# Moving the GpSimd share of the experts' weight subtractions into VectorE's queue

## The chip, the cores and the metric

The kernel runs on one core of one Trainium2 chip. The metric is the device time of one execution in microseconds (us), as a median over runs. The engines are TensorE (PE; its weight loads are PEld), VectorE (DVE), ScalarE (ACT), GpSimd (POOL) and SyncE (SP), which issues most of the DMAs.

## What is computed

The reference is one layer of a hybrid decoder: four kinds of token mixers over 2048 tokens of width 1024, a projection with a layer norm, and then a mixture of experts. The change lies in the experts alone. Each token goes to 2 of 32 SwiGLU experts (width 512), and what they give is weighted and added to the token's row:

```python
def expert_block(args):
    xb, e = args
    return (jax.nn.silu(xb @ w_gate[e]) * (xb @ w_up[e])) @ w_down[e]

y_rows = lax.map(expert_block, (x_rows, block_expert)).reshape(n_rows, d)
y = jax.ops.segment_sum(y_rows * row_gate[:, None], row_tok, num_segments=t_tok + 1)[:t_tok]
```

All data are 32-bit floats.

## The kernel before, in words

The kernel keeps its accuracy with split operands: a float operand is written as a high part `h`, the operand rounded to TensorE's float32r form, and a low part `l = raw - h`, and a product takes three matmuls (high by high, high by low, low by high). For every piece of an expert's weights somebody therefore has to make `h` by a rounding copy (ScalarE) and `l` by a subtraction. The change is about who subtracts.

The mixers, the output projection and the routing take the first two thirds of the time and know nothing of the change. Then `moe` (L1934) runs over the 32 experts in the order of `ORDER`. The weights of one expert come in six raw pieces of 1 MB, each 128 partitions by 2 x 1024 floats: four of gate and up together (`raw_gu`, L1813, two DMAs of 512 KB) and two of the down matrix (`raw_dn`, L1822, one DMA). Raw pieces lie in a pool of five buffers (`m_raw`, L1806). `split_piece` (L1832) handles a piece in two halves of 128x1024: the copy on ScalarE (L1835), then the subtraction on the engine that it is given (L1836). The gate/up parts go to a pool of eight buffers (`m_g`, L1382), which is `h` and `l` of four pieces and so one expert; the down parts go to two buffers each of `m_dh` and `m_dl` (L1807), also one expert. So a piece of the next expert can be split only when TensorE is done with that of the present one.

`load_g` (L1964) lets the last of its pieces be subtracted on GpSimd and the others on VectorE; `load_d` (L1969) lets the first of its two be subtracted on VectorE and the second on GpSimd. An expert thus has eight subtractions on VectorE (six gate/up, two down) and four on GpSimd (two and two). For the first expert two gate/up pieces are prepared earlier, with the routing.

The tokens of an expert are handled in blocks of 128. The first block is always computed; the second under an `If` on the count (over 128), with fewer matmuls when it is at most half full; a third is rare (`third`, L2009, under the `If` of L2011, which TensorE, ScalarE, VectorE and GpSimd all go through). Per expert: the gathered rows are turned by TensorE and split (`transpose_split`, L1400; the transposes are L1408, the split is a ScalarE copy at L51 and a VectorE subtraction at L52, whose input is in PSUM), multiplied with gate and up (`moe_gu`, matmuls L1884), passed through the activation (`moe_h`: ScalarE L1900, VectorE L1901 and L1902; the halves of the second block are folded together before, L1892 and L1893), turned and split again, and multiplied with the down weights (`moe_dn`, matmuls L1916), one expert late. The result is copied out by ScalarE (L1923), with a VectorE step for the second block (L1925), and added to the rows in memory by an indirect storing DMA (`moe_put`, L1930). These stores and the gathers of rows (`moe_gather`, L1840) are issued by GpSimd, in whose queue the subtractions stand too.

The order of the calls in `moe` isn't the order of the queues. When the program is built, the framework's scheduler puts each engine's instructions into an order of its own, by priorities and by its own estimates; nothing moves into or out of an `If`. In the profile the subtractions of L1836 therefore stand between the activation's steps and the splits.

Of the kernel before, what the change touches and what calls it, by code (L numbers as in the profile page):

```python
# [30 lines left out]
class Layer:  # L31
# [1902 lines left out]
    def moe(self, G0=(), x0=None, experts=32):  # L1934
        nc, tc, NB = self.nc, self.tc, self.NB
# [22 lines left out]
        GW, DW, H, Y, cnt = {}, {}, {}, {}, {}  # L1958
# [5 lines left out]
        def load_g(e):  # L1964
            done = list(G0) if e == 0 else []
            R = [self.raw_gu(e, k) for k in range(len(done), 4)]
            GW[e] = done + [self.split_piece((self.g_tile(), self.g_tile()), r, nc.gpsimd if i == len(R) - 1 else nc.vector) for i, r in enumerate(R)]

        def load_d(e):  # L1969
            R = [self.raw_dn(e, k) for k in range(2)]  # L1970
            DW[e] = [self.split_piece(self.d_tiles(), r, g) for r, g in zip(R, (nc.vector, nc.gpsimd))]

        def gather0(e):
            if e < experts:
# [55 lines left out]
        def counts(e):  # L2030
            if e % 4 == 0:
                for t, k, g in ((self.turn_cnt, "pe", [ET.PE]), (self.turn_cnt, "pool", [ET.Pool]), (self.turn_max, "four", FOUR)):
                    for i, v in enumerate(load_counts(t, e, g)):
                        cnt[e + i, k] = v

        load_g(0)
        counts(0)
        if not x0:
# [6 lines left out]
        for e in range(experts):  # L2045
            counts(e + 1)
            if e > 1:
                put1(e - 2)
            third(e - 1)
            gather(e + 1)  # L2050
            gather0(e + 1)
            self.moe_gu(x0, GW[e], b0)
            with tc.If(cnt[e, "pe"] > 128):
                sized(e, 1, lambda s: self.moe_gu(x1, GW[e], b1, half=s))
            H[e, 0] = self.moe_h(b0, gate(e, 0))
            self.fold(b1, half(e, 1))
            H[e, 1] = self.moe_h(b1, gate(e, 1))
            if e + 1 < experts:
                x0 = self.turned(X[0])
                load_g(e + 1)  # L2060
            if e == 31:
                self.lx, self.lp, self.lt = {}, {}, {}
                self.late_x(T - self.LATE)
            if e:
                down0(e - 1, ht[0])
            h0 = turn(e, 0)
            if e:
                down1(e - 1, ht[1])
            ht = h0, turn(e, 1)
            if e + 1 < experts:  # L2070
                x1 = self.turned(X[1], spread=True)
            load_d(e)
        e, t = experts - 1, T - self.LATE
# [316 lines left out]
```

## Time and profile before

| | us |
|---|---|
| median of three runs | 3057.15 (3054.57 to 3073.09) |
| the profiled execution | 3065.59 |
| its span, first to last instruction | 3063.8 |
| of it before the experts | 1975 |
| the experts' stage | 995 |
| behind them (last norm and output) | 94 |

The profile is of one execution. Times in its rows count from the start of the span. "Busy" is the time in which an engine executes; an idle stretch is put down to what ended it. PEclk is the granted share of TensorE's clock, 1.00 for 2.4 GHz and 0.50 for 1.2 GHz.

### The profile page before, as it was taken

What the parts mean: (1) busy time and instruction counts of PE and PEld (TensorE: products, weight loads), DVE (VectorE), ACT (ScalarE), POOL (GpSimd) and SP (SyncE); (2) the same over time, 40 slices, a digit from 0 to 9 for tenths busy, and PEclk for the clock granted to TensorE, in tenths of its full rate; (3) what the DMA queues carried; (4) which work ended last, traced back from release to release, by engine and by line L of the source; (5) the groups of instructions that cost most, each with busy time, mean ns of one, the idle gap of its engine ahead of it and who ended that gap; (6) DMA issues with size and microseconds to landing.
All of it is one profiled execution on the core that took longest, in us unless ns stands there. A gap on an engine that the chain in (4) does not pass through costs nothing. (4 is left out here: it accounts for less than half of the span.)

```text
span 3063.8 us, 42798 instructions
## 1 busy us (share of the span) xinstructions
PE 2826.6 (92%) x15420; PEld 2225.7 (73%) x15421; DVE 1934.6 (63%) x4061; ACT 1225.6 (40%) x2003; POOL 887.9 (29%) x552
## 2 busy tenths in 40 slices
PE   8999999999989999999999999898899888999866
PEld 6898877777867766665577799776677767777644
DVE  6366365366555567776646735677677866667868
ACT  4222132222124423333311112265576656566854
POOL 1000000011010023334431101445464544546524
PEclk9999999999989898989999999999999999999988
DMA  6332242121125422110243412377597767877865
GB/s 189 100 102 71 69 125 70 55 73 56 53 50 164 158 79 80 50 38 18 83 141 136 143 69 70 114 276 259 182 309 233 251 230 230 264 246 244 286 223 195
DMA packets 287042, 442.98 MB, mean 145 GB/s; under 512 B 84088, under 2 KB 152040, under 8 KB 286760
## 3 DMA queue, kind: packets, MB, share of 16 engines
q1 hardware_dynamic: 272200, 397.78, 39.2%
q0 software_dynamic: 14560, 41.47, 5.4%
q8 instruction: 172, 2.82, 0.4%
q14 instruction: 110, 0.90, 0.1%
HBM read 350.52 MB, written 96.50 MB: 146 GB/s over the span
## 5 line engine op out<-in xcount | busy, mean ns | idle before, releaser
L1884 PE MATMUL m_g<-m_g,xhl 128*128 128x512 f32 x2032 | 521.0, 404 | 16.4 <-PEq L2011 9.1
L1884 PEld LDWEIGHTS m_g<-m_g,xhl 128*128 128x128 f32 x2032 | 376.0, 192 | 110.1 <-issue 31.5
L1836 DVE TENSOR_TENSOR m_g<-m_raw,m_g 128x1024 fp32r<-128x1024 f32 x188 | 273.5, 1482 | 109.7 <-ACT m_g L1835 104.4
L1835 ACT CAST m_g<-m_raw 128x1024 fp32r<-128x1024 f32 x252 | 255.4, 1058 | 111.2 <-PEq L2011 99.2
L1916 PE MATMUL m_y<-m_dh,m_h 128*128 128x512 f32 x656 | 225.8, 409 | 24.0 <-PEq L2011 7.3
L59 PE MATMUL pbank<-xh,wh 128*128 128x512 f32 x544 | 226.6, 417 | 6.6 <-DVE us L213 3.6
L60 PE MATMUL pbank<-xl,wh 128*128 128x512 f32 x544 | 218.8, 402 | 0.0
L61 PE MATMUL pbank<-xh,wl 128*128 128x512 f32 x544 | 218.3, 402 | 0.0
L51 ACT CAST xhl<-bank 128x512 fp32r<-128x512 f32 x204 | 118.3, 609 | 240.2 <-PE bank L1408 239.1
L1836 POOL TENSOR_TENSOR m_g<-m_raw,m_g 128x1024 fp32r<-128x1024 f32 x64 | 184.9, 2971 | 84.5 <-ACT m_g L1835 47.5
L1466 PE MATMUL wide<-wt,xhl 128*128 128x512 f32 x768 | 183.2, 397 | 3.6 <-ACT xhl L51 3.6
L1836 POOL TENSOR_TENSOR m_dl<-m_raw,m_dh 128x1024 fp32r<-128x1024 f32 x64 | 178.3, 2819 | 23.9 <-ACT m_dh L1835 23.7
L1304 POOL TENSOR_TENSOR mla_acc<-mla_acc,mla_pt 128x512 f32<-128x512 f32 (+3 forms) x112 | 132.2, 1180 | 147.4 <-ACT mla_pt L1302 137.4
L1466 PEld LDWEIGHTS wide<-wt,xhl 128*128 128x128 f32 x768 | 143.9, 189 | 40.0 <-ACT xhl L51 7.5
L1302 ACT ACTIVATE mla_pt<-sbank 128x512 f32<-128x512 f32 (+3 forms) x160 | 85.3, 533 | 212.6 <-PE sbank L1298 110.8
L1916 PEld LDWEIGHTS m_y<-m_dh,m_h 128*128 128x128 f32 x656 | 128.6, 196 | 57.1 <-issue 10.8
L52 DVE TENSOR_TENSOR xhl<-bank,xhl 128x512 fp32r<-128x512 f32 x204 | 136.2, 684 | 49.9 <-ACT xhl L51 48.0
L1930 POOL DMA_INDIRECT accd<-m_y,m_put x47 | 96.1, 2044 | 247.2 <-ACT m_y L1923 148.1
L59 PE MATMUL pbank<-wh,xh 128*128 128x256 f32 x512 | 151.8, 296 | 0.0
L1646 PE MATMUL gate<-wt,xhl 128*128 128x354 f32 (+1 forms) x864 | 150.3, 331 | 1.1 <-ACT xhl L51 0.9
L60 PE MATMUL pbank<-wl,xh 128*128 128x256 f32 x512 | 150.3, 293 | 0.0
L61 PE MATMUL pbank<-wh,xl 128*128 128x256 f32 x512 | 149.1, 291 | 0.0
(643 smaller groups left out, 6279.6 us busy)
## 6 DMA issues: line engine op xcount, KB each, us to landing
m_raw<-in_moe_w_down SPq DMA_DIRECT2D x64, 1024.0 KB
m_raw<-in_moe_w_gate SPq DMA_DIRECT2D x126, 512.0 KB
m_raw<-in_moe_w_up SPq DMA_DIRECT2D x126, 512.0 KB
wraw<-in_w_in SPq DMA_DIRECT2D x80, 256.0 KB
o_x<-in_x SPq DMA_DIRECT2D x16, 512.0 KB
x1d<-m_g SPq DMA_DIRECT2D x16, 512.0 KB
accd<-wide SPq DMA_DIRECT2D x16, 512.0 KB
m_raw<-accd SPq DMA_DIRECT2D x7, 1024.0 KB
```

The source lines that it names most:

```text
L51: nc.scalar.copy(hi, src)
L52: (eng and nc.gpsimd or nc.vector).tensor_sub(lo, src, hi.bitcast(F32))
L59: nc.tensor.matmul(out, lh, rh, start=start, stop=False)
L60: nc.tensor.matmul(out, lh, rl, start=False, stop=False)
L61: nc.tensor.matmul(out, ll, rh, start=False, stop=stop)
L1304: (nc.vector if kt in self.SUMS else nc.gpsimd).tensor_add(acc[:, c0 * 128:512], acc[:, c0 * 128:512], pt[:, 0:n])
L1466: nc.tensor.matmul(p[:, j], a[:, k], W[k][bb][:, j * 512:j * 512 + 512], start=k == 0 and i == 0, stop=k == 7 and i == 2)
L1646: nc.tensor.matmul(p[:, 0:n], a[:, k], b[:, o:o + n], start=k == 0 and i == 0, stop=k == 7 and i == 2)
L1835: self.nc.scalar.copy(h[:, i], raw[:, i])
L1836: lo_eng.tensor_sub(l[:, i], raw[:, i], h[:, i].bitcast(F32))
L1884: self.mark["pe"] = self.nc.tensor.matmul(banks[:, j], a, b[:, k % 2, j * 512:j * 512 + 512], start=k == 0 and i == 0, stop=k == 7 and i = ...
L1916: self.nc.tensor.matmul(p[:, j], a, b[:, k % 2, j * 512:j * 512 + 512], start=k == 0 and i == 0, stop=k == 3 and i == len(ps) - 1)
```

## The change

All subtractions of the experts' weights go to VectorE: of the last gate/up piece and of the second down piece too. GpSimd keeps the gathers and the adding stores. Nothing else differs.

```diff
         def load_g(e):
             done = list(G0) if e == 0 else []
             R = [self.raw_gu(e, k) for k in range(len(done), 4)]
-            GW[e] = done + [self.split_piece((self.g_tile(), self.g_tile()), r, nc.gpsimd if i == len(R) - 1 else nc.vector) for i, r in enumerate(R)]
+            GW[e] = done + [self.split_piece((self.g_tile(), self.g_tile()), r, nc.vector) for r in R]
 
         def load_d(e):
             R = [self.raw_dn(e, k) for k in range(2)]
-            DW[e] = [self.split_piece(self.d_tiles(), r, g) for r, g in zip(R, (nc.vector, nc.gpsimd))]
+            DW[e] = [self.split_piece(self.d_tiles(), r, nc.vector) for r in R]
```

## Rows read from the trace of the kernel before

**Rows 1.** Stages; from:to, length, busy of PE, PEld, DVE, ACT, POOL, clock, DMA.
```profile
0.00:1975.00 1975.00, 1888.17 (x11204) 1482.50 (x11205) 1156.10 (x3166) 551.18 (x1072) 342.85 (x315) 0.95 0.29 89
1975.00:2970.00 995.00, 884.11 (x4000) 699.65 (x4000) 707.69 (x741) 636.33 (x858) 506.68 (x223) 0.96 0.76 250
2970.00:3063.80 93.80, 54.28 (x216) 43.58 (x216) 70.83 (x157) 38.07 (x74) 38.37 (x16) 0.77 0.55 200
```
**Rows 2.** Groups of the experts' stage; shape, count, busy us, mean ns, idle before and releasers.
```profile
L1836 DVE TENSOR_TENSOR m_g<-m_raw,m_g 128x1024 fp32r<-128x1024 f32 x188 | 273.5, 1482 | 109.7 <-ACT m_g L1835 104.4 <-PE bank L1408 3.2 <-DVEq L2011 1.9
L1835 ACT CAST m_g<-m_raw 128x1024 fp32r<-128x1024 f32 x252 | 255.4, 1058 | 111.2 <-PEq L2011 99.2 <-DMA m_raw<-in_moe_w_down 9.2 <-DMA m_raw<-in_moe_w_up 1.2
...
L1836 POOL TENSOR_TENSOR m_g<-m_raw,m_g 128x1024 fp32r<-128x1024 f32 x64 | 184.9, 2971 | 84.5 <-ACT m_g L1835 47.5 <-issue 37.0
L1836 POOL TENSOR_TENSOR m_dl<-m_raw,m_dh 128x1024 fp32r<-128x1024 f32 x64 | 178.3, 2819 | 23.9 <-ACT m_dh L1835 23.7
...
L1836 DVE TENSOR_TENSOR m_dl<-m_raw,m_dh 128x1024 fp32r<-128x1024 f32 x64 | 114.3, 1786 | 12.3 <-ACT m_dh L1835 12.3
...
L1916 PEld LDWEIGHTS m_y<-m_dl,m_h 128*128 128x128 f32 x360 | 71.0, 197 | 15.3 <-POOL m_dl L1836 1.3
```
**Rows 3.** The subtraction's line, whole run; count, then duration ns least, median, most.
```profile
L1836 DVE TENSOR_TENSOR m_g<-m_raw,m_g x188: 1205/1220/6290, 1983.0 to 2915.4; 128x1024 fp32r<-128x1024 f32 x188
```
**Rows 4.** VectorE's timeline; start, duration, line, count merged: free, then held.
```profile
2406.46 3.49 DVE L1836 TENSOR_TENSOR m_g<-m_raw,m_g 128x1024 fp32r<-128x1024 f32 x3
...
2600.09 8.49 DVE L1836 TENSOR_TENSOR m_g<-m_raw,m_g 128x1024 fp32r<-128x1024 f32 x3
2608.51 0.68 DVE L52 TENSOR_TENSOR m_h<-bank,m_h 128x512 fp32r<-128x512 f32 x1
```
**Rows 5.** GpSimd's timeline in the same stretch.
```profile
2602.20 5.29 POOL L1836 TENSOR_TENSOR m_g<-m_raw,m_g 128x1024 fp32r<-128x1024 f32 x2
```
**Rows 6.** TensorE's timeline; in brackets the idle time before and what ended it.
```profile
2082.95 0.66 PE L1408 MATMUL bank<-ident,m_t 128*128 128x128 f32 x4 [1.85 <-DVE xhl L52]
...
2609.24 1.12 PE L1408 MATMUL bank<-ident,m_xg 128*128 128x128 f32 x4 [4.24 <-DVE m_h L52]
...
2922.31 0.66 PE L1408 MATMUL bank<-ident,m_xg 128*128 128x128 f32 x4 [1.66 <-DVE m_h L52]
```
**Rows 7.** Stretches of half clock behind a wait, columns as in the stages.
```profile
2361.70:2368.50 6.80, 5.67 (x18) 4.82 (x19) 5.91 (x8) 4.90 (x7) 2.77 (x2) 0.50 0.69 233
...
2849.80:2853.20 3.40, 3.40 (x13) 2.87 (x12) 3.31 (x5) 2.18 (x4) 0.00 (x0) 0.50 0.93 290
```
**Rows 8.** Waits of TensorE's weight loads, experts' stage; us in total, times, longest.
```profile
PEld m_g L1884 <- POOL m_g L1836: 4.3, 7, 0.9
```
**Rows 9.** Stretches of one expert each, columns as in the stages.
```profile
2220.80:2245.00 24.20, 23.31 (x112) 18.49 (x111) 19.05 (x22) 18.66 (x25) 15.92 (x8) 1.00 0.90 290
2245.00:2265.70 20.70, 19.89 (x93) 14.81 (x91) 19.79 (x22) 18.27 (x26) 13.02 (x6) 1.00 0.97 313
...
2592.70:2619.70 27.00, 22.17 (x94) 16.98 (x93) 21.85 (x21) 17.57 (x26) 13.36 (x6) 0.87 0.76 259
...
2743.50:2777.70 34.20, 33.64 (x157) 27.25 (x155) 21.53 (x22) 18.38 (x26) 18.84 (x9) 1.00 0.89 296
...
2830.00:2859.20 29.20, 21.49 (x93) 16.13 (x92) 25.27 (x22) 17.51 (x25) 15.40 (x7) 0.94 0.89 283
...
2881.80:2902.50 20.70, 19.81 (x94) 14.96 (x92) 19.78 (x22) 18.28 (x26) 13.85 (x6) 1.00 0.87 301
```
**Rows 10.** Gathers, who waited for them, landings; then the stores.
```profile
L1840 POOL DMA_INDIRECT m_xg<-x1d,m_idx x46: 937/993/1822, 1976.4 to 2883.5; - x46
...
  PE bank L1408: 4.0, 1
...
DMA to landing us min/median/max: 4.2/7.0/10.6
...
L1930 POOL DMA_INDIRECT accd<-m_y,m_put x47: 1562/2106/2687, 2029.3 to 2968.6; - x47
```
**Rows 11.** The subtractions alone, one expert; length, busy of DVE and POOL.
```profile
2245.00:2265.70 20.70, 11.03 (x8) 9.19 (x4) 1.00 0.97 313
```

## The prediction

> **What bounds the kernel now.** I read the stages first. The experts' stage, 1975 to 2970 us, holds TensorE for 884.1 of its 995 us, VectorE for 707.7, ScalarE for 636.3 and GpSimd for 506.7, with the DMA engines at 0.76 [rows 1]. Nothing that the diff touches runs outside it, so the other 2069 us stay. TensorE is the first bound here, but what it lacks is the question: a DMA bound would show as ScalarE's first copies of a piece waiting for landings, and of their 111.2 us of idle time 99.2 end on a branch of TensorE's and only about 10 on a landing [rows 2]. Weights arrive early; they wait for buffers.
>
> Then the groups of the stage. The subtraction of line 1836 runs 252 times on VectorE, 1482 ns each for the gate/up pieces (188) and 1786 ns for the down pieces (64), and 128 times on GpSimd at 2971 and 2819 ns [rows 2]. One shape, one operation, and yet two means on VectorE: the median is 1220 ns, the shortest 1205 and the longest 6290 [rows 3]. A minority of long ones makes the mean. One of them in the timeline: three subtractions take 8.49 us where three others take 3.49 [rows 4], and within these 8.49 us GpSimd runs its pair, 5.29 us [rows 5]. VectorE stands still while GpSimd's subtraction runs, and the one that started first goes on.
>
> What that does to TensorE: at 2609.24 it had waited 4.24 us for the split of line 52 that stands behind the held subtraction in VectorE's queue [rows 6]. Ten such waits follow a held subtraction (1.85, 1.01, 1.20, 3.11, 2.35, 4.24, 1.86, 1.01, 4.24, 1.66; first, largest and last shown), 22.5 us in all. After four of them the granted clock is at 0.5, 1.2 GHz instead of 2.4, for 23.8 us in sum (first and last shown) [rows 7].
>
> **The change, part by part.** *GpSimd loses 128 subtractions*, 184.9 + 178.3 = 363.2 us of its busy time [rows 2]. It is no bound, so that by itself gives nothing. What TensorE waited for GpSimd's pieces goes: 4.3 us at the gate/up weights [rows 8] and 1.3 us at the down weights [rows 2], 5.6 us.
>
> *The holding goes.* VectorE's excess over its median is 188 x 0.262 + 64 x 0.566 = 49.3 + 36.2 = 85.5 us [rows 2, 3]. Of that TensorE felt the 22.5 us above. The four stretches at half clock hold 5.67 + 5.11 + 4.96 + 3.40 = 19.1 us of matmuls (first and last shown) [rows 7], which at full clock would take half: 9.6 us. So at most 22.5 + 9.6 + 5.6 = 37.7 us come back.
>
> *VectorE gets 128 subtractions*, 128 x 1.22 = 156.2 us; less the 85.5 it is 70.7 us busier, 778 of 995 us. By expert that is 4 x 1.22 = 4.88 us. Where does it meet TensorE? In an expert with a second block there is cover: the stretch from 2743.5 lasts 34.2 us with TensorE at 33.64 and VectorE at 21.53 [rows 9], so 4.88 more lie in 12.7 us of idle VectorE. An expert without one has no such cover. The stores of line 1930 number 47 [rows 10]: 32 first blocks and 15 others, two of these third blocks, so 13 experts have a second block and 19 have none. In the stretch from 2245.0, 20.7 us long, VectorE is busy for 19.79 us, 0.956 of it [rows 9], and 11.03 of these are the eight subtractions [rows 11]. Without holding it needs 19.79 - 11.03 + 8 x 1.22 = 18.5 us, with the moved ones 18.5 + 4.88 = 23.4 us, and at the same share of 0.956 the stretch takes 24.5 us. VectorE becomes the bound of a short expert.
>
> So every short stretch under 24.5 us grows to it. There are seven (24.2, 20.7, 20.1, 23.2, 22.3, 22.6, 20.7 us; the first two and the last shown [rows 9]): 0.3 + 3.8 + 4.4 + 1.3 + 2.2 + 1.9 + 3.8 = 17.7 us. And a short stretch that was held can't win more than down to 24.5: from 2592.7 it is 27.0 us [rows 9] and wins 2.5 of the 4.24 + 2.5 it lost; from 2830.0 it is 29.2 [rows 9] and wins 4.7 of 8.8; that from 2075.4 wins 3.6 of 4.1. Not won: 4.2 + 4.1 + 0.5 = 8.8 us.
>
> *Order and waits.* The moved subtractions wait for the same ScalarE copies as before, and behind those copies on ScalarE stand the copies that the next VectorE operations need anyway, so the wait for a late piece adds little; what is added is the 2.4 us of a pair ahead of a split or a scaling. This is the 4.88 us above and is not counted again. In the queues of the loads (SP) nothing is added: raw buffers come free after 2.4 us of VectorE instead of 5.3 to 5.9 us of GpSimd, so loads start earlier, and since landings hardly end a wait [rows 2] I take nothing for it (bounds: 10 us of landing waits gained, or the same again lost to closer traffic). GpSimd's gathers and stores no longer stand behind subtractions; the one wait for a gather was 4.0 us, for the first [rows 10], so I take nothing (at best those 4.0 us, at worst the last rival). The scheduler orders all queues anew with the changed list; the trace has no row for that. Its bounds: the largest wait seen, 4.24 us [rows 6], gained or lost in every fourth expert, 34 us either way; I take 0, since nothing speaks for a side.
>
> Sum: 37.7 - 17.7 - 8.8 = 11.2 us less. The profiled execution took 3065.6 us (span 3063.8 and 1.8 around it) and would come to 3054.4; it lies 8.4 us above the median of the three runs, 3057.15, and against that median I say 3046 us.
>
> **A rule weighed.** The gathers take 0.993 us in the middle and at most 1.822, the stores 1.562 to 2.687 [rows 10], so something already stretches them by about a microsecond. The Trainium skill's "SBUF — State Buffer", section "SBUF: two separate sides", says that a DMA issued by GpSimd can't get its descriptors written while VectorE runs in a mode that uses both of its ports; its section "Who interferes with whom" takes TENSOR_TENSOR out of this, by inference, and leaves only the reading side shared. By the first, more subtractions on VectorE would slow the gathers (the fourth rival); by the second they don't. The trace bears the second out better, since VectorE's subtractions are stretched to 6.29 us [rows 3] and the gathers by 0.8 at most.
>
> **Rivals.** *All cover (faster).* The short experts are not paced by VectorE, because work in the next heavy one lends it time: pieces for later can be prepared in idle stretches. Then the 37.7 us come whole: 3057.15 - 37.7 = 3019.5 us. For it: 12.7 us idle VectorE in heavy stretches. Against: there are eight buffers for gate/up halves, one expert's worth, so preparation can't run ahead.
>
> *VectorE paces every short expert (slower).* All four moved subtractions fall ahead of the split of line 52 or the scalings of lines 1901 and 1902 that TensorE waits for, in all 19 short experts: 19 x 4.88 = 92.7 us, against the 37.7: 55 us more, 3112 us. It is slower than before from the point where over 37.7 of the 92.7 us reach TensorE, and by over 1% from 68.3. For it: VectorE at 0.956 in a short stretch [rows 9]. Against: stretches at 25 us and more have some slack, and ScalarE's copies pace part of it.
>
> *Nothing (the change is absorbed).* Gain and cost meet within 5 us: 3057 us. It lies in my forecast's own range and has no chance of its own.
>
> *Gathers starved.* Each expert's first gather is late by one subtraction, 32 x 1.22 = 39 us on top of the forecast: 3085 us. Against: a landing takes 7.0 us and one wait alone ended on one [rows 10]. By the first section of the rule weighed above it would go this way.
>
> **How the numbers follow.** The forecast with its own range, 3028 to 3066 us, gets 0.5; all cover 0.25; VectorE paces 0.2; starved gathers 0.05. About 1%, 30.6 us, is what a measurement of this kernel can tell. The all-cover case lies mostly beyond it (3019.5 against 3026.6), with a little of the forecast: 0.25. VectorE paces gives 0.2 slower and starved gathers a little: 0.22. The rest, 0.53, is within 1%. The range reaches from 3010, all cover with the 10 us of landings in part, to 3092, half way into the slower rival.
>
> **What would show it.** Right: no GpSimd subtraction, VectorE's line 1836 380 times with a mean near 1.22 us and none over 2 us; its busy time in the stage up by 60 to 80 us; no half clock after a held subtraction; short stretches near 24 us with VectorE over 0.93 busy and new waits of TensorE for the split of line 52 or for line 1902. Wrong: short stretches that stay at 20 to 21 us (all cover), TensorE's waits on VectorE grown past 68 us (VectorE paces), waits of the transposes on gathers, or subtractions that stay long with no GpSimd work beside them, which would mean that the holding has another cause.

## The result, and the profile after

Nine runs of the changed kernel gave a median of 3079.19 us (3056.48 to 3101.04) against 3057.15 us for nine of the kernel before: a ratio of 1.0076, with a 95% interval of 1.0051 to 1.0102. The forecast was 3046 us, 11 us less than before; it became some 23 us more. One execution among all those below, of 4957.17 us at a mean granted clock of 0.833, is left out of its kernel's ratio. The profiled execution took 3078.34 us with a span of 3076.6, 12.75 us more than that of before. The stages (from:to, length, busy us of PE, PEld, DVE, ACT and POOL, clock, DMA) show where:

```profile
0.00:1979.00 1979.00, 1888.96 (x11204) 1481.49 (x11205) 1159.49 (x3166) 551.40 (x1072) 342.77 (x316) 0.95 0.29 89
1979.00:2984.00 1005.00, 886.85 (x4000) 714.91 (x4000) 763.34 (x869) 640.95 (x858) 143.54 (x94) 0.94 0.76 248
2984.00:3076.60 92.60, 52.67 (x216) 41.95 (x216) 70.76 (x157) 38.13 (x74) 38.51 (x16) 0.79 0.55 203
```

Against [rows 1] the experts' stage is 10 us longer, 1005 for 995; the 4 us before it contain nothing of the change. GpSimd fell from 506.7 to 143.5 us, VectorE rose from 707.7 to 763.3, and the mean granted clock went from 0.96 to 0.94.

The subtraction's own rows, first the durations (ns least, median, most), then the groups of the stage (busy us, mean ns, idle before):

```profile
L1836 DVE TENSOR_TENSOR m_g<-m_raw,m_g x252: 1205/1218/1228, 1986.6 to 2933.0; 128x1024 fp32r<-128x1024 f32 x126
L1836 DVE TENSOR_TENSOR m_dl<-m_raw,m_dh x128: 1210/1216/1221, 2015.4 to 2960.6; 128x1024 fp32r<-128x1024 f32 x128
```

```profile
L1836 DVE TENSOR_TENSOR m_g<-m_raw,m_g 128x1024 fp32r<-128x1024 f32 x252 | 298.1, 1219 | 73.3 <-ACT m_g L1835 72.5
...
L1836 DVE TENSOR_TENSOR m_dl<-m_raw,m_dh 128x1024 fp32r<-128x1024 f32 x128 | 150.4, 1216 | 0.0
```

The holding is gone to the last instance: no subtraction takes over 1.228 us, where [rows 3] had 6.290. So the change does what it says, and what it was to gain has to be lost elsewhere. Now what TensorE waits for in the stage (us in total, times, longest):

```profile
PE m_y L1916 <- DVEq L2011: 44.2, 14, 3.8
PE bank L1408 <- DVEq L2011: 11.1, 6, 2.6
```

DVEq L2011 is VectorE's queue at the end of the third block's `If`. The down product behind that `If` writes the same PSUM tile (`m_y`) as the block in it, so it can start only when VectorE has left the `If`, and VectorE leaves it only when the work queued ahead of it is finished. In the kernel before, the profile has 0.9 us of the first wait and none of the second; but it puts three waits of the transposes down to "issue", which means that it names no releaser, and the example below shows that the longest of them ended at this branch too:

```profile
PE bank L1408 <- issue: 6.1, 3, 3.1
...
PE m_y L1916 <- DVEq L2011: 0.9, 1, 0.9
```

One expert shows the exchange. VectorE, before, around 2356 us (start, duration; in brackets idle time and its releaser), with its step out of the `If` (count, durations in ns, first and last start), and TensorE behind it:

```profile
2355.74 6.93 DVE L1836 TENSOR_TENSOR m_dl<-m_raw,m_dh 128x1024 fp32r<-128x1024 f32 x1
```

```profile
L2011 DVEq EVENT_SEMAPHORE  x2: 21/21/21, 2362.7 to 2362.8; - x2
```

```profile
2362.83 0.44 PE L1408 MATMUL bank<-ident,m_xg 128*128 128x128 f32 x1 [3.11 <-issue]
```

And the same expert in the changed kernel:

```profile
2372.93 3.48 DVE L1836 TENSOR_TENSOR m_dl<-m_raw,m_dh 128x1024 fp32r<-128x1024 f32 x3
2376.34 0.68 DVE L1901 SCALAR_TENSOR_TENSOR m_t<-m_t,m_g 128x512 f32<-128x512 f32 x1
```

```profile
2377.22 0.47 PE L1916 MATMUL m_y<-m_dh,m_h 128*128 128x512 f32 x1 [3.14 <-DVEq L2011]
```

Before, a held subtraction of 6.93 us ends at 2362.67 and TensorE goes on at 2362.83, after 3.11 us. After, three subtractions without any holding and the activation's product end at 2377.02 and TensorE goes on at 2377.22, after 3.14 us. The wait has changed its name and kept its length. In many other experts, where nothing had been held, such a wait is new. This expert as a whole became shorter all the same: the wait before was followed by the half clock of [rows 7] from 2361.7, the wait after by none. The expert before, then after:

```profile
2359.80:2392.20 32.40, 29.37 (x128) 24.28 (x129) 24.09 (x23) 18.64 (x26) 17.02 (x9) 0.89 0.77 248
2375.10:2404.20 29.10, 26.98 (x129) 22.47 (x130) 24.87 (x29) 19.37 (x26) 5.07 (x3) 1.00 0.88 285
```

### The profile page after: what moved, and what is told of

Same layout as the page of the kernel before. It is cut to its first block, busy times and chain, and to the rows that moved or that the text cites. A ratio compares the mean times of both kernels' runs of the same rounds, so it can differ in the third digit from the quotient of the medians.

```text
span 3076.6 us, 42685 instructions
## 1 busy us (share of the span) xinstructions
PE 2828.5 (92%) x15420; PEld 2238.4 (73%) x15421; DVE 1993.6 (65%) x4189; ACT 1230.5 (40%) x2003; POOL 524.8 (17%) x424
## 5 line engine op out<-in xcount | busy, mean ns | idle before, releaser
L1884 PE MATMUL m_g<-m_g,xhl 128*128 128x512 f32 x2032 | 506.8, 399 | 7.7 <-PEq L2011 2.8
L1836 DVE TENSOR_TENSOR m_g<-m_raw,m_g 128x1024 fp32r<-128x1024 f32 x252 | 298.1, 1219 | 73.3 <-ACT m_g L1835 72.5
L1916 PE MATMUL m_y<-m_dh,m_h 128*128 128x512 f32 x656 | 234.4, 423 | 62.0 <-DVEq L2011 44.2
L1916 PEld LDWEIGHTS m_y<-m_dh,m_h 128*128 128x128 f32 x656 | 135.0, 206 | 100.7 <-issue 42.0
L1916 PE MATMUL m_y<-m_dl,m_h 128*128 128x512 f32 x360 | 152.1, 423 | 0.0
L1836 DVE TENSOR_TENSOR m_dl<-m_raw,m_dh 128x1024 fp32r<-128x1024 f32 x128 | 150.4, 1216 | 0.0
```

Of the source, the lines that this page charges most:

```text
L1836: lo_eng.tensor_sub(l[:, i], raw[:, i], h[:, i].bitcast(F32))
L1884: self.mark["pe"] = self.nc.tensor.matmul(banks[:, j], a, b[:, k % 2, j * 512:j * 512 + 512], start=k == 0 and i == 0, stop=k == 7 and i = ...
L1916: self.nc.tensor.matmul(p[:, j], a, b[:, k % 2, j * 512:j * 512 + 512], start=k == 0 and i == 0, stop=k == 3 and i == len(ps) - 1)
```

## The experiments

The theories at first: theory 1, *the way to the branch* (the moved down pair and the product L1901 stand ahead of the third block's `If` in VectorE's queue and delay its exit); theory 2, *VectorE's load* (each added microsecond counts); theory 3, *order alone* (L1901 ahead of the branch, where the changed lists let the scheduler put it: in 23 of 31 passes, in the kernel before in none). Theory 4 came later. Where order counts below, it is that of the compiled queues. Each ratio is to the kernel before, in runs on the same chip.

**One half each.** Only the gate/up piece moved (shown, against the changed kernel: the down piece goes back to GpSimd), or only the down piece (the kernel before with the same line turned round):

```diff
-            DW[e] = [self.split_piece(self.d_tiles(), r, nc.vector) for r in R]
+            DW[e] = [self.split_piece(self.d_tiles(), r, g) for r, g in zip(R, (nc.vector, nc.gpsimd))]
```

> Only the last gate/up piece is moved to VectorE; the second down piece stays with GpSimd. Theory 1 (the way to the branch): the cost of the change is what stands in VectorE's queue ahead of the third block's branch, since TensorE's first down matmul behind it waits until VectorE has passed; the moved down pair is the larger part of that, and here it is absent. The held gate/up subtractions are gone (49 us of VectorE's excess), the activation's step of line 1901 stands ahead of the branch in 23 passes: about 3045 to 3062 us, against 3057 before. Theory 2 (VectorE's load): a short expert is paced by VectorE's total, and half the moved work costs half: about 3068. Theory 3 (order alone): the step of line 1901 ahead of the branch is the cost, and it is there as in the changed kernel: about 3075.

> Only the second down piece is moved to VectorE; the last gate/up piece stays with GpSimd. Theory 1: the moved pair stands ahead of the third block's branch in every pass, the cost is all there and only the smaller part of the holding (36 us of VectorE's excess) goes: 3080 to 3095 us. Theory 2: half of the cost, about 3068. Theory 3: as the changed kernel, about 3075.

Measured: gate/up alone 3089.7 us, 1.0073 [1.0045, 1.0100]; down alone 3066.23 us, 0.9987 [0.9966, 1.0008]. Theory 1 had put the cost on the down pair, and it falls in that form; theory 3 as the only cause falls too, since L1901 stands ahead of the branch in 23 passes of both. Theory 2, as "each half costs half", fails as well, until one counts VectorE's time with the holding in it. The groups of the two kernels, gate/up alone first, then down alone:

```profile
L1836 DVE TENSOR_TENSOR m_g<-m_raw,m_g 128x1024 fp32r<-128x1024 f32 x252 | 298.4, 1219 | 122.7 <-ACT m_g L1835 116.0 <-DMA m_raw<-in_moe_w_down 5.7
L1836 DVE TENSOR_TENSOR m_dl<-m_raw,m_dh 128x1024 fp32r<-128x1024 f32 x64 | 144.5, 2257 | 0.0
```

```profile
L1836 DVE TENSOR_TENSOR m_g<-m_raw,m_g 128x1024 fp32r<-128x1024 f32 x188 | 227.8, 1243 | 9.4 <-ACT m_g L1835 8.4
L1836 DVE TENSOR_TENSOR m_dl<-m_raw,m_dh 128x1024 fp32r<-128x1024 f32 x128 | 175.8, 1415 | 4.9 <-ACT m_dh L1835 4.9
```

Both added 64 instructions. But with the gate/up piece moved, GpSimd's down pair goes on holding VectorE's down pair (2257 ns mean), and the subtractions sum to 298.4 + 144.5 = 442.9 us, where those of before came to 273.5 + 114.3 = 387.8 [rows 2]. With the down piece moved they sum to 227.8 + 175.8 = 403.6. One half adds 55 us to VectorE and costs 0.7%, the other adds 16 us and costs nothing.

**The holding alone.** As before, but GpSimd writes zeros instead of subtracting, so the low parts of the pieces on GpSimd are left out:

```diff
-            lo_eng.tensor_sub(l[:, i], raw[:, i], h[:, i].bitcast(F32))
+            lo_eng.memset(l[:, i].bitcast(F32), 0.0) if lo_eng is self.nc.gpsimd else lo_eng.tensor_sub(l[:, i], raw[:, i], h[:, i].bitcast(F32))
```

> Who does what is as before, but where GpSimd subtracted it now only writes zeros: the low parts of the last gate/up piece and of the second down piece are left out. It reads nothing and takes about 1 us for each half instead of 2.9. If a reading GpSimd is what holds VectorE, no subtraction of VectorE's takes over 2 us, and the holding's price is what the time falls by: 25 to 38 us by the working ahead of the result, 3019 to 3032. If VectorE's long subtractions have another cause they stay and the time is near 3057.

Measured: 3022.85 us, 0.9845 [0.982, 0.987]. GpSimd is as present in the queues as before, but reads nothing:

```profile
L1836 DVE TENSOR_TENSOR m_g<-m_raw,m_g x188: 1204/1217/1228, 1988.6 to 2884.3; 128x1024 fp32r<-128x1024 f32 x188
...
L1836 POOL MEMSET m_g<- x64: 972/1554/1596, 1983.1 to 2883.2; 128x1024 f32 x64
L1836 POOL MEMSET m_dl<- x64: 949/1551/1575, 2009.5 to 2907.0; 128x1024 f32 x64
```

No VectorE subtraction is held beside 128 writes of GpSimd: it is GpSimd's reading that holds. (The Trainium skill's "SBUF — State Buffer", section "Who interferes with whom", says that a VectorE instruction with two SBUF inputs contends with a GpSimd instruction that reads SBUF and not with one that only writes it; both rows agree.) The holding, with the waits for GpSimd's slow pieces, is worth 1.55%, about 47 us (GpSimd's writes also took 1.55 us where its subtractions took 2.9; that isn't told apart). So the gain side of the forecast stood, and the loss had to be larger than the 23 us net: 1.0076 - 0.9845 = 0.0231, about 71 us for the 128 subtractions on VectorE.

**L1901 behind the branch.** The changed kernel with one order fixed in VectorE's queue (an ordering edge, no wait):

```diff
-            third(e - 1)
+            third(e - 1); behind = self.mark["dve"].ins.name
...
-            H[e, 0] = self.moe_h(b0, gate(e, 0))
+            H[e, 0] = self.moe_h(b0, gate(e, 0)); tc.add_manual_dep(self.mark["dve"].ins, behind, mybir.DependencyInfo(mybir.DependencyClass.NoSync, mybir.DependencyReason.DATA), reason="behind the third block")
```

> The changed kernel with one more order: the first activation step of line 1901 stands behind the third block's branch in VectorE's queue, as it does in the kernel before; all subtractions stay on VectorE. Theory 1: TensorE's wait at the branch loses that step and its wait for ScalarE, 0.7 to 1.5 us in each of the some 16 short experts, the moved pair stays: 3060 to 3072 us. Theory 2: no change, about 3079. Theory 3: the cost is gone and the freed holding shows, 3045 or less.

Measured: 3070.56 us, 1.0016 [0.9993, 1.0039]. The place of that one product seemed to be worth 0.6%, 18 us, in this kernel: nearly all of the net loss, and a quarter of the 71 us. TensorE's waits at the branch hardly fall with it, to 47.3 us (17 times) from 55.3 (20). I kept it as a share to be tested again.

**Theory 4, the bare branch.** In the kernel before 4.9 first-block matmuls stand on average between the second block's branch and the third block's in TensorE's queue, in the changed kernel 1.0 (none in 24 of 32 passes), and TensorE's own branch took up to 2.46 us there (though up to 4.49 us in the kernel before). I thought that this lost cover was the loss. The kernel before with all first-block matmuls ahead of the second block's (so none between; `self.gus` lists the gate/up matmuls as they are made):

```diff
-            self.moe_gu(x0, GW[e], b0)
+            self.moe_gu(x0, GW[e], b0); n = len(self.gus)
...
-                sized(e, 1, lambda s: self.moe_gu(x1, GW[e], b1, half=s))
+                sized(e, 1, lambda s: self.moe_gu(x1, GW[e], b1, half=s)); [tc.add_manual_dep(m.ins, self.gus[n - 1].ins.name, mybir.DependencyInfo(mybir.DependencyClass.NoSync, mybir.DependencyReason.DATA), reason="behind the first block") for m in self.gus[n:]]
```

> The kernel before, with one order fixed in TensorE's queue: all first-block gate and up matmuls of an expert stand ahead of its second block's branch. In the kernel before, 0 to 9 of them (4.9 on average, none in 1 of 32 passes) stand between the second block's branch and the third block's; in the changed kernel none does in 24 passes of 32. VectorE's, ScalarE's and GpSimd's work is as before. Theory 4, new (the bare branch: TensorE has to drain at the end of the second block's branch and then fetch for the third block's branch for up to 2.6 us, and what hides this is the few matmuls queued between the two): TensorE's idle time from 1 us before to 7 us after the third block's branch, 37 us in all before, goes up by about 34 us as it did with the change (to 72), the half-clock time there from 34 to about 80 us, and the time by 25 to 55 us, 1.008 to 1.018 of before. Theories 1 and 3 (VectorE's queue ahead of the branch) and theory 2 (VectorE's load): no difference, 0.998 to 1.002.

The other way round, the last six of them (`last = self.gus[-6:]`) pinned behind the second block's branch, in the changed kernel, in the changed kernel with L1901 pinned too, and in the kernel before:

```diff
-                sized(e, 1, lambda s: self.moe_gu(x1, GW[e], b1, half=s))
+                sized(e, 1, lambda s: self.moe_gu(x1, GW[e], b1, half=s)); [tc.add_manual_dep(m.ins, self.mark["pe"].ins.name, mybir.DependencyInfo(mybir.DependencyClass.NoSync, mybir.DependencyReason.DATA), reason="behind the second block") for m in last]
```

> The changed kernel, with the last six first-block gate and up matmuls of each expert pinned in TensorE's queue behind its second block's branch, so that six stand between the two branches in 31 of 32 passes. The gate's product L1901 and both down pairs stand ahead of the third block's branch in VectorE's queue as in the changed kernel (23 of 32). Theory 4: idle time near the branch falls from 72 back to about 40 us, and what is left is the gain elsewhere (25.7 us of idle time and 12.6 us of half clock less than before): 25 to 35 us faster than before, 0.988 to 0.993. Theory 1 or 3 (L1901 and the down pairs ahead of the branch): 0.4 to 0.8% slower than before, as the changed kernel is. Theory 2 (VectorE's load): as the changed kernel, 1.006 to 1.010.

> The changed kernel with both: the six matmuls between the branches, and L1901 behind the third block's branch as in the run before (after_pin, which gave 1.0016). Theory 4: as with the six matmuls alone, or up to 10 us better: 0.985 to 0.992. Theories 1 and 3: as after_pin, 1.000 to 1.004. Theory 2: 1.001 to 1.004, as after_pin.

> The kernel before with the same pin of six matmuls: between the branches stand 5 to 9 where it had 0 to 9 (6.3 on average for 4.9). A control for what the pin does without the change. Theory 4: the idle time near the branch falls a little from its 37 us, the time by 0 to 10 us: 0.997 to 1.000, so that the changed kernel with the pin is 0.8 to 1.2% faster than this one. Theories 1 to 3: 0.998 to 1.002, and the changed kernel with the pin is slower than this one.

Measured: the cover taken from the kernel before 3049.41 us, 0.9943 [0.9921, 0.9965]; six matmuls of cover in the changed kernel 3091.47 us, 1.0081 [1.0060, 1.0102]; with L1901 pinned too 3084.15 us, 1.0059 [1.0030, 1.0087]; the control 3064.62 us, 0.9990 [0.9971, 1.0009]. Theory 4 is wrong with the sign reversed: without the cover the kernel before gets faster, and with it the changed kernel gains nothing. TensorE's waits of the changed kernel with the cover say why:

```profile
PE m_y L1916 <- DVEq L2011: 50.1, 17, 4.9
PE bank L1408 <- DVEq L2011: 14.3, 6, 3.4
```

TensorE isn't late with its own branch there, it waits for VectorE's exit all the same. And the kernel before without the cover has less holding: its subtractions sum to 238.2 + 119.2 = 357.4 us for 387.8. It is faster than both kernels, and 30.4 us less on VectorE would account for it at half a microsecond each; why GpSimd's pairs meet VectorE's less often in this order is not shown.

**VectorE's time, varied.** In the kernel with GpSimd's zeros nothing holds VectorE, so its time can be set. Its subtractions for the first two gate/up pieces of each expert are done twice (or for the first piece only), in the middle of the queue, on pieces that arrived long ago:

```diff
-    def split_piece(self, hl, raw, lo_eng):
+    def split_piece(self, hl, raw, lo_eng, n=1):
...
-            lo_eng.memset(l[:, i].bitcast(F32), 0.0) if lo_eng is self.nc.gpsimd else lo_eng.tensor_sub(l[:, i], raw[:, i], h[:, i].bitcast(F32))
+            lo_eng.memset(l[:, i].bitcast(F32), 0.0) if lo_eng is self.nc.gpsimd else [lo_eng.tensor_sub(l[:, i], raw[:, i], h[:, i].bitcast(F32)) for _ in range(n)]
...
-            GW[e] = done + [self.split_piece((self.g_tile(), self.g_tile()), r, nc.gpsimd if i == len(R) - 1 else nc.vector) for i, r in enumerate(R)]
+            GW[e] = done + [self.split_piece((self.g_tile(), self.g_tile()), r, nc.gpsimd if i == len(R) - 1 else nc.vector, 1 + (i < 2)) for i, r in enumerate(R)]
```

> As the run in which GpSimd writes zeros instead of subtracting (no_read, 0.9845 of before), but VectorE does the subtractions of the first two gate and up pieces of each expert twice: some 126 instructions of 1.22 us, 153 us of VectorE work with the same result, in the middle of its queue, on pieces that have long arrived. VectorE's busy time over the 32 passes then is about 609 + 153 = 762 us (750 in the changed kernel, 696 in the kernel before, of which some 77 us is holding). Theory 2 (what counts is the time VectorE needs for an expert, held or working): as the changed kernel, 1.003 to 1.010. Theory 1 (what counts is what stands in VectorE's queue right ahead of the third block's branch): at most half of the loss comes back, 0.985 to 0.993.

> Between no_read (0.9845) and no_read_twice (1.0070): VectorE does the subtractions of only the first gate and up piece of each expert twice, some 62 instructions of 1.22 us, 76 us. If each microsecond of VectorE costs alike (theory 2): half way, 0.993 to 0.998, with VectorE's subtractions at about 380 us in the 32 passes, like the kernel before with its pin (382 us, 0.999). If VectorE's time is free up to a point (the forecast's way of counting, by which an expert pays only where VectorE's need passes its stretch): 0.984 to 0.990, most of the loss lying in the second half.

Measured: two pieces twice 3084.16 us, 1.0070 [1.0043, 1.0097]; one piece twice 3057.59 us, 0.9979 [0.9952, 1.0005]. The first is as slow as the changed kernel, without one subtraction moved and with nothing held. Its rows:

```profile
L1836 DVE TENSOR_TENSOR m_g<-m_raw,m_g 128x1024 fp32r<-128x1024 f32 x314 | 367.8, 1219 | 45.1 <-ACT m_g L1835 24.0 <-issue 20.2
L1836 DVE TENSOR_TENSOR m_dl<-m_raw,m_dh 128x1024 fp32r<-128x1024 f32 x64 | 76.0, 1216 | 0.0
```

```profile
PE m_g L1884 <- DVE m_g L1836: 33.5, 21, 2.2
PE m_y L1916 <- DVEq L2011: 24.6, 15, 1.9
```

VectorE's subtractions go from 301.1 us (223.6 + 77.5, nothing done twice) through 375.2 to 443.8 us, and the time from 0.9845 through 0.9979 to 1.0070: 41 us for the first 74.1, 28 us for the next 68.6. On average a microsecond of VectorE costs about half a microsecond here: 0.0225 x 3064 / 142.7 = 0.48. The forecast's picture, free up to a point and then a bound, would have had most of the loss in the second half. TensorE meets the lateness elsewhere than in the changed kernel, more of it at the gate/up pieces themselves.

Two other things moved with the doubling. One is the order: by VectorE's records L1901 stands ahead of the branch in none of the 27 passes that skip the third block with the zeros alone, in 10 with one piece twice, in 18 with two. With L1901 pinned behind it the second point stays (1.0087, the last runs below), so that point doesn't need it; the first one is not told apart. The other is the loads: a doubled subtraction keeps its raw buffer longer, and ScalarE's copies of the down pieces then wait for landings, 13.1 us with one piece twice and 34.2 us with two, a wait that neither the zeros alone nor the kernels before and changed have:

```profile
ACT m_dh L1835 <- DMA m_raw<-in_moe_w_down: 34.2, 23, 4.5
```

So 0.48 can hold some late loading, and no run takes that out. What needs no doubling is the direct price: with the zeros and the changed kernel, 71 us for the 147.4 us that VectorE has more in L1836, and 52 us (1.0016 - 0.9845) with L1901 pinned: 0.48 and 0.36.

**Without the branch.** Theory 1 in its last form was that the exit of the third block's `If` is what lets VectorE's lateness through. Both kernels without third blocks:

```diff
-            third(e - 1)
...
-        third(e)
```

> The kernel before without the third block of any expert, and so without its branch (the tokens of third blocks are left out). To be set against the same edit on the changed kernel. Both theories: shorter than before by the third blocks' own work, 0.955 to 0.985.

> The changed kernel without the third blocks and their branch. If VectorE's lateness reaches TensorE only where TensorE's down product waits for VectorE at that branch (theory 1, and the place that the trace shows), nothing is left of the loss, and the changed kernel is 0.8 to 1.3% faster than the kernel before with the same cut. If a longer VectorE counts wherever its results are read (theory 2 alone), the changed kernel stays 0.3 to 1.0% slower than the other with the same cut.

Measured: 2997.87 us (0.9795 [0.9765, 0.9826]) and 3004.23 us (0.9825 [0.9795, 0.9855]); the change costs 3004.23 / 2997.87 = 1.0021 there (0.9825 / 0.9795 = 1.0031 by the ratios, whose intervals overlap), neither the gain of theory 1 nor clearly the loss of theory 2. VectorE's rows say why. Changed and unchanged, both without third blocks:

```profile
L1836 DVE TENSOR_TENSOR m_g<-m_raw,m_g 128x1024 fp32r<-128x1024 f32 x252 | 296.8, 1218 | 50.4 <-ACT m_g L1835 50.1
L1836 DVE TENSOR_TENSOR m_dl<-m_raw,m_dh 128x1024 fp32r<-128x1024 f32 x128 | 148.6, 1216 | 0.0
```

```profile
L1836 DVE TENSOR_TENSOR m_g<-m_raw,m_g 128x1024 fp32r<-128x1024 f32 x188 | 318.5, 1743 | 26.5 <-ACT m_g L1835 25.9 <-DMA m_raw<-in_moe_w_down 0.4
L1836 DVE TENSOR_TENSOR m_dl<-m_raw,m_dh 128x1024 fp32r<-128x1024 f32 x64 | 107.7, 1683 | 0.0
```

Without third blocks the unchanged kernel is held more (426.2 us instead of 387.8), so the change adds only 445.4 - 426.2 = 19.2 us to VectorE, and at 0.48 that is 9 us, 0.3%, in line with what was measured. So the gain that theory 1 foretold here isn't there, while a loss of 0.3% is not clear of noise. Without the branch TensorE waits for the subtractions directly (24.1 us at the gate/up matmuls, 18.6 us at the down matmuls).

**What was left.** The down half alone together with the order that had made the kernel before faster, and two more pairs that differ in the place of L1901 alone:

> Only the down weights' second piece goes to VectorE (d_only, 0.9987), and the first block's gate and up matmuls all stand ahead of the second block's branch in TensorE's queue (the order that made the kernel before 0.57% faster). Theory 2: VectorE's busy time is some 30 us below that of d_only, 680 us, and the two gains add up in part: 0.988 to 0.995. Theory 1 (the down pair is ahead of the branch in VectorE's queue): 0.997 to 1.002.

> As no_read_twice (1.0070), with the first activation's product L1901 pinned behind the third block's branch in VectorE's queue, where no_read_twice has it ahead in 22 of 31 passes. If its place costs on its own (theory 3, as a share beside theory 2): 0.999 to 1.003, as the pin did in after_pin. If VectorE's time alone counts: 1.005 to 1.009.

> As the run with only the gate and up pieces moved (g_only, 1.0073), with L1901 pinned behind the third block's branch (ahead in 23 of 31 passes without the pin). Theory 3 as a share: 1.000 to 1.004. VectorE's time alone: 1.005 to 1.009.

Measured: 3062.71 us, 1.0004 [0.9980, 1.0028]; 3086.13 us, 1.0087 [1.0059, 1.0115]; 3067.99 us, 1.0023 [0.9999, 1.0047]. The order doesn't help the down half, whose subtractions stay at 230.1 + 176.4 = 406.5 us: it never was a gain by itself, and the expected 680 us of VectorE was mistaken. The pin gives nothing in the kernel with doubled subtractions and 0.5% in the other. All runs but the two without third blocks, by VectorE's time in L1836 (profiled execution of each):

| kernel | L1836 on VectorE, us | ratio |
|---|---|---|
| GpSimd writes zeros | 301.1 | 0.9845 |
| before, no matmuls between the branches | 357.4 | 0.9943 |
| zeros, one piece twice | 375.2 | 0.9979 |
| before, cover pinned | 379.3 | 0.9990 |
| before | 387.8 | 1 |
| down piece moved | 403.6 | 0.9987 |
| the same, no matmuls between | 406.5 | 1.0004 |
| gate/up piece moved | 442.9 | 1.0073 |
| the same, L1901 pinned | 443.9 | 1.0023 |
| zeros, two pieces twice | 443.8 | 1.0070 |
| the same, L1901 pinned | 443.6 | 1.0087 |
| the change | 448.5 | 1.0076 |
| the same, L1901 pinned | 448.6 | 1.0016 |
| the same, cover pinned | 448.3 | 1.0081 |
| the same, both pinned | 448.4 | 1.0059 |

At 0.48 us for each the rows fall within their intervals or just beside them, but for the down piece moved (0.9987 where 1.0025 would follow) and two of the four kernels with L1901 pinned. A second effect of the queue's order is therefore real in those, of up to 0.6%, and 0.48 is an average: the four kernels with GpSimd's part moved and nothing held lie between 1.0016 and 1.0081 at the same 448 us. Why the pin works in two kernels and hardly or not in the others stays open.

## Why the prediction was wrong

**The holding** was read rightly. It is gone, as foreseen (none over 2 us; 380 subtractions; mean 1.219 and 1.216 us). Its worth was put at 37.7 us and measured, with GpSimd's zeros, at about 47; the terms named for it were 80% of that.

**VectorE's added time** was counted nearly rightly: 70.7 us forecast for the stage (60 to 80 as the sign of being right), 55.6 measured (763.3 - 707.7), 60.7 in L1836 alone.

**The cost of it is the step that failed.** "VectorE becomes the bound of a short expert", and so 17.7 us in seven stretches, with 4.88 us covered in every longer one. Measured for the same 128 subtractions: about 71 us (0.0231 of 3064) where the forecast had 17.7 + 8.8 = 26.5; half of the added VectorE time reaches TensorE, in long experts too. Even with L1901 pinned back it is 52 us, twice the forecast. In the short stretches themselves the step did fairly: of two of [rows 9] of 20.7 us, forecast at 24.5, that from 2245.0 became 24.0 and that from 2881.8 became 21.5:

```profile
2257.90:2281.90 24.00, 21.19 (x96) 17.13 (x96) 22.00 (x26) 19.53 (x26) 4.30 (x3) 0.93 0.90 297
2896.50:2918.00 21.50, 21.20 (x94) 17.05 (x93) 20.34 (x23) 17.16 (x23) 3.25 (x2) 0.88 0.84 285
```

Most of it lies in the others. A longer expert, before and after, each from one test of the third block's branch by TensorE to the next:

```profile
2617.30:2646.10 28.80, 28.30 (x135) 22.90 (x134) 21.21 (x22) 19.39 (x26) 18.08 (x10) 1.00 0.80 271
```

```profile
2623.70:2655.70 32.00, 28.82 (x127) 23.96 (x128) 25.49 (x30) 19.47 (x26) 4.90 (x3) 0.89 0.85 270
```

```profile
2626.88 0.76 PE L1916 MATMUL m_y<-m_dh,m_h 128*128 128x512 f32 x1 [3.84 <-DVEq L2011]
```

VectorE was busy for 21.2 of 28.8 us, so by the forecast's rule 4.88 more had room in 7.6 idle ones; the expert took 3.2 us more, and the one new wait of TensorE in it, 3.84 us (the last fence), ends on VectorE at the branch. Cut in this way at all 32 passes, 11 are shorter by 25.2 us in all (the first three, 5.4, 5.2 and 4.7, are those with the holding of [rows 4] at 2600, of 2355 above, and of the stretch from 2830.0), 20 are longer by 33.5, and of these 33.5 only 8.2 lie in the five passes that had been under 25 us. The reading of the rows, which no run tests by itself: the room was idle time of an engine that works through its queue in order. It lies where VectorE waits for ScalarE's copies (104.4 us ahead of the gate/up subtractions [rows 2]), and these wait for TensorE to come to the branch and free the buffers (99.2 us [rows 2]). Behind the branch of one expert the copies begin, then the subtractions, and before the next branch all of them must be through. Added work moves the end of that chain; it does not slide into the holes ahead of it.

**The unequal prices.** The forecast priced a microsecond of holding at 37.7 / 85.5 = 0.44 us of time and an added one at (17.7 + 8.8) / 156 = 0.17. The runs give both a price of the same size: 47 us for the 86.7 us that go with GpSimd's zeros, 0.55, and 0.48 for the moved ones, 0.36 with L1901 pinned. With one price of 0.48 the sign follows from [rows 2] alone: 85.5 us of holding go, 156.2 us of work come, and 70.7 x 0.48 is 34 us more.

**Order and waits**, taken at 0 with bounds of 34 us either way: the scheduler did put L1901 ahead of the branch in 23 passes of 31, and pinning it back gave 0.6%, 18 us, though not in all kernels. That is within its bounds and a smaller part of the 71 us than the load, but not nothing: with the pin the change costs 5 us in all, and its interval (0.9993 to 1.0039) doesn't tell that from none.

**The rivals.** "VectorE paces every short expert" had the right sign, at 55 us instead of 23, and an engine's lateness as its mechanism, but in the wrong place (short experts only, all of it). That 3079 us lies between 3010 and 3092 is owed to this rival alone, which had widened the range; the forecast's mechanism has no part in it. "All cover" is refuted by the cost of the moved subtractions. Starved gathers didn't happen: the gathers took 932/994/1793 ns and the stores 1546/2146/2503 (least, median, most) beside 380 subtractions, where [rows 10] had 937/993/1822 and 1562/2106/2687; so the slow gathers that were drawn from the Trainium skill's "SBUF — State Buffer", section "SBUF: two separate sides", aren't seen, and the exception for TENSOR_TENSOR in its section "Who interferes with whom" agrees with these rows. The half clock that was to go with the holding came back behind the new waits (0.94 for 0.96 in the stage); the doubled kernel is as slow at 0.96, and TensorE's busy time for the same 4000 matmuls rose by only 2.7 us (886.85 for 884.11), so it isn't the main cause.

## What to carry to other kernels

Give a price of one size to all time of an engine that works in order on a chain that another engine waits for: what it lost to a neighbour's holding and what it did itself weighed about the same here. Before moving work to free it of a holding, compare the time that is held with the time that is added; here 85 us were traded for 156. And idle share is no cover: look at whether the idle time lies ahead of the added work's inputs or behind them, and test the price by doing some of the work twice, with an eye on the buffers that the doubled work holds longer and on the order that the scheduler makes of it.

## What was not expected of the hardware

GpSimd's writes leave VectorE's subtractions alone completely (128 of them, no subtraction over 1.228 us), while its reads stretch them up to 6.93 us. And the `If` of the third block, entered for few experts, has its price in many of the others: an engine leaves it only when its queue ahead of it is finished, and the next user of a tile that the `If` touches waits for that, 20 times and 55.3 us in the changed kernel; VectorE's test of the branch itself took 0.05 to 0.07 us.
